# Third and fourth block of a depthwise convolution begun on ScalarE and summed by transfers, and one store on another queue, in a Trainium2 hybrid encoder block

## The chip, the cores and the metric

The kernel runs on one core of one Trainium2 chip, in one launch. The metric is device time in microseconds (us). The engines are named as in the profile: PE is TensorE (its weight loads are PEld), DVE is VectorE, ACT is ScalarE, POOL is GpSimd, SP is SyncE, whose queue starts most loads and stores. Each engine works through its own instructions in the order in which the program lists them, and waits where an operand is not there yet.

## What is computed

One layer of a streaming encoder on 512 tokens of 1,024 channels in fp32: a half-step feed-forward layer, one joint projection whose output feeds a convolution module and a gated linear attention, an output projection, a second half-step feed-forward layer, a gated embedding, and a last norm. The change touches the convolution, in the middle:

```python
def _conv_module(a, b, w_dw, b_dw, ln_g, ln_b):
    glu = a * jax.nn.sigmoid(b)
    y = lax.conv_general_dilated(
        glu, w_dw[:, None, :], window_strides=(1,),
        padding=((CONV_WIDTH - 1, 0),), dimension_numbers=("NWC", "WIO", "NWC"),
        feature_group_count=D_CONV) + b_dw
    return jax.nn.silu(_layernorm(y, ln_g, ln_b))
```

There are 512 channels and a width of 31: each output token is the bias plus 31 products of a channel's own weights with its tokens up to 30 back. The layer norm runs over the 512 channels, so it needs all of them. Beside it the attention works in chunks of 64 tokens with 4 heads; its output is normalised for each head and multiplied by the swish of a gate `r`. Both outputs meet in the output projection `w_out`.

## The kernel before

Channels lie on the 128 partitions, tokens along the row, so the convolution's 512 channels are four blocks of 128 channels by 512 tokens. `glu[c]` is the input of block c and `acc[c]` its accumulator (tiles `cv`). A block is 31 instructions on VectorE (`conv_steps`, lines 1013 to 1020): one `tensor_scalar` that takes the tap without delay and adds the bias, then 30 `scalar_tensor_tensor`, tap w over 512 - (30 - w) columns, which add a product to the accumulator, from 482 columns up to 511. `taps(n)` hands out n such steps at a fixed place in the program, alternating between the two oldest blocks that are not finished. A block that turns out to be finished is dropped, and that call of `taps` counts as one of the n without an instruction. So the taps fill VectorE's time between other work, and the order is written out by hand: PE, DVE and ACT run in the program's order there (`in_order(True)`). GpSimd is not held to that order in this stretch; the scheduler places its instructions.

What stands around the convolution, in order: the projection's blocks for the convolution (`zblock`), whose last gate and value make `glu[3]`; the projections q and k; the tokens' value rows (`tokblock(wv, t)`, tiles `v`); `scores` of the attention, between whose parts `taps((6, 4)[j])` stands and for which GpSimd clears tiles `sc`; then the gate's rows (`tokblock(wr, t)`). After the second of these come 15 taps, the head norm's square sums `so`, and the norm `rso = rsqrt_mean(so, ...)`: a mean `ms` on DVE, its power -1/2 on POOL (`rs<-ms,negh`), five taps, and a Newton step on DVE. ACT multiplies the attention's four token blocks with it (`ytok[i]`, 128 tokens each; the tiles are called `r` or `y` in the profile, after the buffer they share), and DVE multiplies them by the gate's `rt[i]`:

```python
        if t == 3:
            acc012 = bt(s="acc012")
            dve.tensor_tensor(out=acc012, in0=acc[0], in1=acc[1], op=ALU.add)
        if t > 0:
            taps((0, 2, 5, 1)[t])
            for i in {1: (0,), 2: (1, 2), 3: (3,)}[t]:
                dve.tensor_tensor(out=ytok[i], in0=ytok[i], in1=rt[i], op=ALU.mult)
```

TensorE then transposes `ytok[0]` to `ytok[3]` in this order (`ps<-ident,y`), with two products for the later embedding (`sm,px`) ahead of the last. `yg` are the transposed rows scaled, the inputs of `w_out`. All steps of the convolution that are left are run behind `yg`; `acc012`, the sum of the four accumulators (tile `r` in the profile), is multiplied by a constant matrix on TensorE (`ps<-r,mean`), which gives the layer norm's mean.

Products in three parts need each weight split in a rounded part (`wh`, on ACT) and a rest (`wl`). For `added(...)` the rest is made without DVE: ACT writes the negated rounded part and a transfer from POOL's queue adds the weight to it (`accum_op=ALU.add`). Such transfers stand in POOL's queue, and a transfer that waits holds up what is behind it. Weights come through six buffers that SP's loads fill in turn.

At the end each of the four token blocks is stored in two halves of 256 KB (`put`). All go out from SP's queue except `scaled_out(1, 0, ...)`, which is issued on ACT's.

Of the kernel before, what the change touches and what calls it, by code (L numbers as in the profile page):

```python
# [11 lines left out]
AF = mybir.ActivationFunctionType  # L12
ALU = mybir.AluOpType
PSUM = bass.MemoryType.PSUM

P = 128
SEQ = 512
# [4 lines left out]
WIDTH = 31  # L22
PAD = WIDTH - 1
# [39 lines left out]
def block_kernel(ctx: ExitStack, tc: tile.TileContext, a: dict, out: bass.AP):  # L63
    nc = tc.nc
    pe, dve, act, pool = (Ordered(tc, e) for e in (nc.tensor, nc.vector, nc.scalar, nc.gpsimd))
# [15 lines left out]
    def nm(s):  # L81
        uid[0] += 1
        return f"{s}_{uid[0]}"
# [6 lines left out]
    def bt2(dt=F32R, s="a"):  # L90
        t = big.tile([P, 2, SEQ], dt, tag="A", bufs=NA, name=nm(s))
        hi, lo = t[:, 0], t[:, 1]
        whole_of[id(hi)] = hi, t
        return hi, lo

    def bt(dt=F32, s="a"):
        if dt not in other:
            t, other[dt] = bt2(dt, s)
            return t
        return other.pop(dt)  # L100

    def cvt(dt=F32, s="cv"):
        return big.tile([P, SEQ], dt, tag="CV", bufs=NCV, name=nm(s))

    def tmp(s, w=SEQ, dt=F32, bufs=2):
        return tp.tile([P, w], dt, tag=s, bufs=bufs, name=nm(s))
# [20 lines left out]
    def bank():  # L127
        if mode[0] == 0:
            turn_no[0] += 1
            at = turn_no[0] % 7  # L130
            if at in (3, 4):
                return fixed()
            if at in (5, 6):
                return spare()
        return psum(singles(), 3, [P, SEQ])
# [36 lines left out]
    cw = col[:, ncol - DC:]  # L172
# [5 lines left out]
    def vec(name, c, n=1):  # L178
        at = first_of[name] + c
        return col0[:, at:at + n] if at < DC else col[:, at - DC:at - DC + n]  # L180
# [37 lines left out]
    def load(src, k0, nk, c0, ncol):  # L218
        r3 = raw(nk, ncol)
        fetch(r3, src, k0, nk, c0, ncol)  # L220
        return r3

    def high(r3):

        nk, nc_ = r3.shape[1], r3.shape[2]
        hi = wp.tile([P, 1024], F32R, tag="wh", bufs=6, name=nm("wh"))
        lo = wp.tile([P, 1024], F32R, tag="wl", bufs=6, name=nm("wl"))
        h3 = hi[:, :nk * nc_].rearrange("p (k c) -> p k c", k=nk)
        l3 = lo[:, :nk * nc_].rearrange("p (k c) -> p k c", k=nk)
        act.copy(h3, r3)  # L230
        return h3, l3, r3
# [6 lines left out]
    def added(w):  # L238

        h3, l3, r3 = w  # L240
        act.mul(l3, r3, -1.0)
        pool.dma_start(out=l3.bitcast(F32), in_=r3, accum_op=ALU.add)
        return w
# [5 lines left out]
    def mm3(ps, wh, wl, xh, xl, first, last):  # L249
        pe.matmul(ps, wh, xh, start=first, stop=False)  # L250
        pe.matmul(ps, wh, xl, start=False, stop=False)
        pe.matmul(ps, wl, xh, start=False, stop=last)
# [15 lines left out]
    def rows_of(w, k):  # L268

        part, kk = (w[k // 4], k % 4) if isinstance(w, list) else (w, k)  # L270
        return part[0][:, kk, :], part[1][:, kk, :]

    def zblock(w, x, mid={}):

        ps = bank()
        for k in range(DC):
            if k in mid:
                mid[k]()
            wh, wl = rows_of(w, k)
            mm3(ps, wh, wl, *x[k], k == 0, k == DC - 1)  # L280
        return ps
# [728 lines left out]

    glu, acc, conv = [], [cvt() for _ in range(4)], []

    def conv_steps(c):
        y, g, tap = acc[c], glu[c], cw[:, c * WIDTH:(c + 1) * WIDTH]
        dve.tensor_scalar(y, g, tap[:, PAD:WIDTH], vec("conv_b", c), ALU.mult, ALU.add)
        yield
        for w in range(PAD):
            late = PAD - w
            dve.scalar_tensor_tensor(out=y[:, late:], in0=g[:, 0:SEQ - late], scalar=tap[:, w:w + 1],
                                     in1=y[:, late:], op0=ALU.mult, op1=ALU.add)  # L1020
            yield
# [3 lines left out]
    def taps(n):  # L1025

        for _ in range(n):
            if not conv:
                return
            i = turn[0] % min(2, len(conv))  # L1030
            turn[0] += 1
            try:
                next(conv[i])
            except StopIteration:
                conv.pop(i)
# [8 lines left out]
    def glu_value(ps):  # L1044
        a1 = tmp("u1")
        dve.tensor_tensor(out=a1, in0=ps, in1=rsb, op=ALU.mult)
        return a1

    def glu_out(a1, sg):
        g = bt(s="glu")  # L1050
        dve.tensor_tensor(out=g, in0=a1, in1=sg, op=ALU.mult)
        glu.append(g)
        conv.append(conv_steps(len(glu) - 1))
# [77 lines left out]
    cums, epos, eneg, edec, decay, ends = [], [], [], [], [], []  # L1131
    taps(10)
    glu_out(glu_value(pa), sg)
    pb = zblock(w2b[1], hg)
    taps(5)
    for j in range(2):
# [40 lines left out]
    def k_out(j, ps):  # L1177
        for lst, e in ((kdec, edec), (kneg, eneg), (kpos, epos)):
            t = bt(s="k")
            dve.tensor_tensor(out=t, in0=ps, in1=e[j], op=ALU.mult)  # L1180
            lst.append(t)
# [12 lines left out]
    raw_r = [load(a["w_rows"], k, 2, SEQ, SEQ) for k in (0, 2)]  # L1194
# [14 lines left out]
    def tokblock(w, t, mid={}):  # L1209

        ps = bank()
        ts = slice(t * P, (t + 1) * P)
        i = 0
        for k in range(DC):
            wh, wl = w[k // 2][:2]
            xh, xl = hg[k]
            for x, y in ((xh, wh), (xl, wh), (xh, wl)):
                if i in mid:
                    mid[i]()
                pe.matmul(ps, x[:, ts], y[:, k % 2, :], start=(i == 0), stop=(i == 3 * DC - 1))  # L1220
                i += 1
        return ps
# [6 lines left out]
    def scores(j, between):  # L1229
        p4s = [bank().rearrange("p (u c t) -> p u c t", u=2, t=CH) for _ in range(2)]  # L1230
        ss = []
        for i in range(2):
            s = bt(s="sc").rearrange("p (c t) -> p c t", t=P)
            pool.memset(s, 0.0)
            ss.append(s)
        for u, (kk, qq) in enumerate(((kneg[j], qdec[j]), (kpos[j], qneg[j]))):
            for c in range(0, NCH, 2):
                for i in range(2):
                    d = slice(i * HK, (i + 1) * HK)
                    for cc in (c, c + 1):  # L1240
                        s0 = (cc % 2) * CH
                        cs = slice(cc * CH, (cc + 1) * CH)
                        pe.matmul(p4s[i][s0:s0 + CH, u, c // 2, :], kk[d, cs], qq[d, cs], start=True, stop=True)
        hs = [slice(i * CH, (i + 1) * CH) for i in range(2)]
        for s, p4 in zip(ss, p4s):
            for h in hs:
                act.copy(s[h, :, h], p4[h, 0])
        between()
        for s, p4 in zip(ss, p4s):
            for h in hs:  # L1250
                dve.copy_predicated(s[h, :, h], mask[h], p4[h, 1])
        sc.extend(ss)
# [59 lines left out]
    vt, kdt, wr = [], [], []  # L1312
    for t in range(TB):
        ps = tokblock(wv, t, {8: lambda: wr.append(high(raw_r[2])),
                             14: lambda: wr.append(high(raw_r[3]))} if t == 3 else {})
        if t == 0:
            wr += [added(high(raw_r[i])) for i in range(2)]
            k_out(1, k1)
            taps(3)
        elif t == 1:  # L1320
            taps(4)
        elif t == 2:
            taps(3)
        else:
            taps(5)
            low(wr[2])
            taps(2)
            low(wr[3])
        v = bt(s="v")
        act.activation(v, ps, AF.Copy, scale=rs2[:, t:t + 1])  # L1330
        vt.append(v)
        if t == 1:
            for j in range(2):
                scores(j, lambda: taps((6, 4)[j]))
            for j in range(2):
                kp = bank()
                for i in range(TB):
                    pe.transpose(kp[:, i * P:(i + 1) * P], kdec[j][:, i * P:(i + 1) * P], ident)
                kd = bt(s="kdt")
                act.copy(kd, kp)  # L1340
                kdt.append(kd)
# [47 lines left out]
    for t in range(TB):  # L1389
# [21 lines left out]
        if t == 1:  # L1411
# [4 lines left out]
            for i in range(TB):  # L1416
                y = bt(s="y")
# [114 lines left out]
    for k in range(4):  # L1532
        for n in range(3):
            w, ps = half[n]
# [199 lines left out]
    hf, hl = {}, {}  # L1734
# [77 lines left out]
        dve.scalar_tensor_tensor(out=q, in0=r, scalar=nh, in1=r, op0=ALU.mult, op1=ALU.mult)  # L1812
        dve.scalar_tensor_tensor(out=q, in0=q, scalar=1.5, in1=r, op0=ALU.add, op1=ALU.mult)

    def scaled_out(t, e, src, *queue):
        y = bt(s="y")
        act.activation(y, src, AF.Copy, scale=roots[t][2])
        put(t, e, y, *queue)

    def put(t, e, y, queue=nc.sync):  # L1820
        queue.dma_start(out=out[0, t * P:(t + 1) * P, e * SEQ:(e + 1) * SEQ], in_=y)

    def first_half(t, e):
        y = bt(s="y")
# [116 lines left out]
    root(1)  # L1941
    first_half(0, 0)
    scaled_out(0, 1, gained)
    newton(1)
    scaled_out(1, 0, hf[1], act)
    second_half(1, 1)


# [48 lines left out]
```

## Time and profile before

| what | value |
|---|---|
| time, median of 3 runs | 921.92 us (921.84 to 922.2) |
| time of the profiled execution | 921.48 us |
| span of the profiled execution | 919.7 us |
| granted TensorE clock, mean | 0.998 |
| DVE busy, 380 to 480 us | 19.45 to 19.93 of each 20 us |
| ACT busy, 380 to 480 us | 8.19 to 15.82 of each 20 us |

The span runs from the first to the last instruction; the execution's time is 1.8 us longer than it. A line of a timeline gives start, length (us), engine, line, operation, operands, and in brackets the idle time before it and what ended it. All compute instructions pass through one helper, so they have its line, L46, and are told apart by their operands: `cv<-glu,col,cv` is a tap of the second or third block, `cv<-en,col,cv` one of the fourth, whose `glu` shares a buffer named `en`.

### The profile page before, as it was taken

What the parts mean: (1) busy time and instruction counts of PE and PEld (TensorE: products, weight loads), DVE (VectorE), ACT (ScalarE), POOL (GpSimd) and SP (SyncE); (2) the same over time, 40 slices, a digit from 0 to 9 for tenths busy, and PEclk for the clock granted to TensorE, in tenths of its full rate; (3) what the DMA queues carried; (4) which work ended last, traced back from release to release, by engine and by line L of the source; (5) the groups of instructions that cost most, each with busy time, mean ns of one, the idle gap of its engine ahead of it and who ended that gap; (6) DMA issues with size and microseconds to landing.
All of it is one profiled execution on the core that took longest, in us unless ns stands there. A gap on an engine that the chain in (4) does not pass through costs nothing.

```text
span 919.7 us, 12838 instructions
## 1 busy us (share of the span) xinstructions
PE 910.7 (99%) x4948; PEld 779.7 (85%) x4948; DVE 816.7 (89%) x1090; ACT 511.7 (56%) x746; POOL 60.3 (7%) x76
## 2 busy tenths in 40 slices
PE   9999999999999999999999999999999999999996
PEld 8899888888888887788887889888888888888885
DVE  6699989999989766999996779899999999997896
ACT  7755354445454574463665875455445444556884
POOL 0120000000000111001130020000000000000121
PEclk9999999999999999999999999999999999999999
DMA  9534333224334692245572563333223322358454
GB/s 350 186 100 136 117 112 122 91 73 135 115 92 115 158 295 51 69 118 158 139 166 93 137 157 97 115 116 126 87 84 130 122 89 87 118 155 240 92 99 131
DMA packets 37149, 118.89 MB, mean 129 GB/s; under 512 B 4192, under 2 KB 4960, under 8 KB 37088
## 3 DMA queue, kind: packets, MB, share of 16 engines
q1 hardware_dynamic: 30176, 97.22, 31.8%
q0 software_dynamic: 6624, 20.58, 12.5%
q8 instruction: 39, 0.64, 0.3%
q10 hardware_dynamic: 288, 0.27, 0.1%
q14 instruction: 22, 0.18, 0.1%
HBM read 96.43 MB, written 2.10 MB: 107 GB/s over the span
## 4 chain that ended last, share of the span: by engine, by line
PE 96%; DVE 2%; ACT 1%; issue 0%; POOLq 0%
PE ps L46 56%; PE pd L46 40%; DVE cv L46 1%; ACT wa L46 0%; ACT sq L46 0%; DVE yg L46 0%; DVE r L46 0%; DVE y L46 0%; ACT r L46 0%; ACT sm L46 0%; ACT px L46 0%; POOLq L1993 0%; ACT s L46 0%; DVE u L46 0%; DVE g L46 0%
## 5 line engine op out<-in xcount | busy, mean ns | idle before, releaser
L46 DVE TENSOR_TENSOR wl<-wr,wh 128x1024 fp32r<-128x1024 f32 (+2 forms) x159 | 185.9, 1179 | 16.9 <-ACT wh L46 16.4
L46 ACT CAST wh<-wr 128x1024 fp32r<-128x1024 f32 (+2 forms) x177 | 175.4, 1023 | 14.4 <-PE ps L46 7.7
L46 PE MATMUL pd<-hg,wh 128*128 128x512 f32 x576 | 150.0, 391 | 0.0
L46 PE MATMUL ps<-act,wh 128*128 128x512 f32 x448 | 137.9, 389 | 0.0
L46 PEld LDWEIGHTS pd<-hg,wh 128*128 128x128 f32 x576 | 105.9, 188 | 21.1 <-DVE u L46 0.4
L46 PE MATMUL ps<-hg,wh 128*128 128x512 f32 (+1 forms) x448 | 117.0, 345 | 0.0
L46 PEld LDWEIGHTS ps<-act,wh 128*128 128x128 f32 x448 | 84.1, 188 | 17.5
L46 ACT ACTIVATE s<-g 128x512 f32<-128x512 f32 x48 | 30.4, 632 | 117.6 <-DVE g L46 117.6
L46 PE MATMUL pd<-t,wh 128*128 128x512 f32 x392 | 95.3, 391 | 0.0
L46 ACT COPY sq<-pd 128x1024 f32<-128x1024 f32 x45 | 45.8, 1017 | 86.7 <-PE pd L46 52.3
L46 PE MATMUL ps<-act,wl 128*128 128x512 f32 x224 | 87.1, 389 | 0.0
L46 PEld LDWEIGHTS ps<-hg,wh 128*128 128x128 f32 x448 | 78.0, 190 | 10.5 <-issue 0.5
L46 PEld LDWEIGHTS pd<-t,wh 128*128 128x128 f32 x392 | 71.4, 189 | 13.4
L46 PE MATMUL pd<-hg,wl 128*128 128x256 f32 (+1 forms) x544 | 81.5, 289 | 0.0
L46 PEld LDWEIGHTS pd<-hg,wl 128*128 128x128 f32 x544 | 73.9, 191 | 5.1
L46 PE MATMUL ps<-hg,wl 128*128 128x512 f32 (+1 forms) x224 | 77.0, 344 | 0.0
L46 ACT CAST wh<-sm 128x1024 fp32r<-128x1024 f32 x42 | 44.0, 1050 | 55.6 <-DVE sm L46 50.1
L46 DVE TENSOR_TENSOR wl<-sm,wh 128x1024 fp32r<-128x1024 f32 x42 | 51.0, 1219 | 5.1 <-ACT wh L46 5.1
L46 DVE TENSOR_TENSOR sq<-pd,sq 128x1024 f32<-128x1024 f32 x45 | 54.8, 1218 | 0.4 <-PE pd L46 0.4
L46 PE MATMUL ps<-wh,hg 128*128 128x512 f32 x176 | 54.4, 390 | 0.0
L46 PE MATMUL pd<-t,wl 128*128 128x256 f32 x392 | 52.4, 283 | 0.0
L46 PEld LDWEIGHTS pd<-t,wl 128*128 128x128 f32 x392 | 50.6, 191 | 1.5
(300 smaller groups left out, 1625.2 us busy)
## 6 DMA issues: line engine op xcount, KB each, us to landing
wr<-in_ffn_w_in SPq DMA_DIRECT2D x84, 512.0 KB, 3.6
wr<-in_ffn_w_out SPq DMA_DIRECT2D x32, 512.0 KB, 3.6
wl<-wr POOLq DMA_DIRECT2D x20, 512.0 KB, 5.4
wr<-in_ffn_w_out SPq DMA_DIRECT2D x16, 384.0 KB, 3.3
wr<-in_w_blocks SPq DMA_DIRECT2D x12, 512.0 KB, 5.7
wr<-in_w_rows SPq DMA_DIRECT2D x8, 512.0 KB, 3.8
wr<-in_w_out SPq DMA_DIRECT2D x8, 512.0 KB, 5.9
wq<-in_ple_w_gate SPq DMA_DIRECT2D x8, 512.0 KB, 4.3
```

Of the source, the lines that this page charges most:

```text
L46: inst = call(*args, **kwargs)
```

## The change

`taps_begin` lets ACT write the biased tap into `acc[2]` and `acc[3]`. `taps_apart` lets ACT write the product of one tap into a tile of its own, and `taps_add` adds such a tile to another or to the accumulator by a transfer from POOL's queue. `APART` says how many taps of each block are done so: two for the third, five for the fourth. `conv_steps` leaves these out. Separately, `scaled_out(1, 0, ...)` is now issued on SP's queue like the others.

```diff
+    def taps_apart(c, w, y):
+        late = PAD - w
+        act.activation(y[:, late:], glu[c][:, 0:SEQ - late], AF.Copy, scale=cw[:, c * WIDTH + w:c * WIDTH + w + 1])
+        return y
+    def taps_begin(c):
+        act.activation(acc[c], glu[c], AF.Identity, bias=vec("conv_b", c), scale=cw[:, c * WIDTH + PAD:(c + 1) * WIDTH])
+    def taps_add(y, x, w):
+        pool.dma_start(out=y[:, PAD - w:], in_=x[:, PAD - w:], accum_op=ALU.add)
+    APART = (0, 0, 2, 5)
     def conv_steps(c):
         y, g, tap = acc[c], glu[c], cw[:, c * WIDTH:(c + 1) * WIDTH]
-        dve.tensor_scalar(y, g, tap[:, PAD:WIDTH], vec("conv_b", c), ALU.mult, ALU.add)
-        yield
-        for w in range(PAD):
+        if not APART[c]:
+            dve.tensor_scalar(y, g, tap[:, PAD:WIDTH], vec("conv_b", c), ALU.mult, ALU.add)
+            yield
+        for w in range(APART[c], PAD):
...
     glu_out(glu_value(pa), sg)
+    taps_begin(2)
+    ta = [taps_apart(2, w, bt(s="ta")) for w in range(2)]
+    taps_add(ta[1], ta[0], 0)
+    taps_add(acc[2], ta[1], 1)
     pb = zblock(w2b[1], hg)
...
         if t == 0:
-            wr += [added(high(raw_r[i])) for i in range(2)]
+            wr.append(added(high(raw_r[0])))
+            taps_begin(3)
+            ta = [taps_apart(3, w, tmp(("g1", "u1", "s")[w])) for w in range(3)]
+            taps_add(acc[3], ta[0], 0)
+            taps_add(ta[2], ta[1], 1)
+            wr.append(added(high(raw_r[1])))
+            ta += [taps_apart(3, w, tmp(("g1", "u1")[w - 3])) for w in (3, 4)]
+            taps_add(acc[3], ta[3], 3)
+            taps_add(ta[4], ta[2], 2)
             k_out(1, k1)
             taps(3)
...
                 scores(j, lambda: taps((6, 4)[j]))
+                if j == 0:
+                    taps_add(acc[3], ta[4], 4)
...
-    scaled_out(1, 0, hf[1], act)
+    scaled_out(1, 0, hf[1])
```

The numbers of taps that each `taps(n)` hands out are as they were, and so is the order of TensorE's instructions. On VectorE every tap of the third block moves up by three and of the fourth by six. The first place shown is VectorE between the head norm's last step and the multiplication of `ytok[3]`. There `cv_3195` is the third block's accumulator, `cv_3196` the fourth's, the last column the columns of the tap; `r<-r,st` multiplies `ytok[0]`, the three `y` rows multiply `ytok[1]`, `ytok[2]` and `ytok[3]`, and `r<-cv_3193,cv_3194` adds the first two accumulators. Before:

```order
L46 SCALAR_TENSOR_TENSOR cv_3196<-en_3562,col,cv_3196 128x498
L46 SCALAR_TENSOR_TENSOR cv_3195<-glu_3512,col,cv_3195 128x509
L46 TENSOR_TENSOR r_4271<-r_4271,st_4123 128x512
L46 SCALAR_TENSOR_TENSOR cv_3196<-en_3562,col,cv_3196 128x499
L46 SCALAR_TENSOR_TENSOR cv_3195<-glu_3512,col,cv_3195 128x510
L46 SCALAR_TENSOR_TENSOR cv_3196<-en_3562,col,cv_3196 128x500
L46 SCALAR_TENSOR_TENSOR cv_3195<-glu_3512,col,cv_3195 128x511
L46 SCALAR_TENSOR_TENSOR cv_3196<-en_3562,col,cv_3196 128x501
L46 TENSOR_TENSOR y_4297<-y_4297,r_4271 128x512
L46 TENSOR_TENSOR y_4297<-y_4297,y_4306 128x512
L46 TENSOR_TENSOR r_4372<-cv_3193,cv_3194 128x512
L46 TENSOR_TENSOR y_4306<-y_4306,r_4372 128x512
```

At the same place on VectorE, in the changed kernel:

```order
L46 SCALAR_TENSOR_TENSOR cv_3196<-en_3568,col,cv_3196 128x504
L46 TENSOR_TENSOR r_4293<-r_4293,st_4145 128x512
L46 SCALAR_TENSOR_TENSOR cv_3196<-en_3568,col,cv_3196 128x505
L46 SCALAR_TENSOR_TENSOR cv_3196<-en_3568,col,cv_3196 128x506
L46 SCALAR_TENSOR_TENSOR cv_3196<-en_3568,col,cv_3196 128x507
L46 SCALAR_TENSOR_TENSOR cv_3196<-en_3568,col,cv_3196 128x508
L46 SCALAR_TENSOR_TENSOR cv_3196<-en_3568,col,cv_3196 128x509
L46 TENSOR_TENSOR y_4319<-y_4319,r_4293 128x512
L46 TENSOR_TENSOR y_4319<-y_4319,y_4328 128x512
L46 TENSOR_TENSOR r_4393<-cv_3193,cv_3194 128x512
L46 SCALAR_TENSOR_TENSOR cv_3196<-en_3568,col,cv_3196 128x510
L46 TENSOR_TENSOR y_4328<-y_4328,r_4393 128x512
```

One tap fewer stands ahead of `ytok[0]`, the five behind it are all of the fourth block, and one tap stands ahead of `ytok[3]` that was not there. The second place is GpSimd from the attention's value rows on. Before (`wl` are rests of weights, `sc` the cleared tiles):

```order
L46 DMA wl_3591<-wr_3346 128x1024
L46 DMA wl_3805<-wr_3688 128x1024
L46 DMA wl_3810<-wr_3690 128x1024
L46 MEMSET sc_3855 128x512 x2
L46 MEMSET sc_3906 128x512 x2
```

At the same place on GpSimd, in the changed kernel (`g`, `u` and `s` are the partial products of the fourth block):

```order
L46 DMA wl_3811<-wr_3694 128x1024
L46 DMA cv_3196<-g_659_3816 128x482
L46 DMA s_3820<-u_660_3818 128x483
L46 DMA wl_3825<-wr_3696 128x1024
L46 DMA cv_3196<-g_664_3829 128x485
L46 DMA u_665_3831<-s_3820 128x484
L46 MEMSET sc_3876 128x512 x2
L46 MEMSET sc_3928 128x512 x2
L46 DMA cv_3196<-u_665_3831 128x486
```

Four adding transfers now stand ahead of the memsets, and a fifth behind them. The third place is GpSimd around the head norm's power. Before (`px` and `sm` belong to the later embedding, `wa` to `w_out`):

```order
L46 DMA wl_4047<-wr_4042 128x1024
L46 DMA wl_4052<-wr_4044 128x1024
L46 DMA px_4041<-u_680_4038 128x256
L46 TENSOR_TENSOR rs_710_4256<-ms_4254,negh 128x16
L46 DMA sm_4234<-wr_4036 128x1024
```

At the same place on GpSimd, in the changed kernel:

```order
L46 DMA wl_4069<-wr_4064 128x1024
L46 DMA wl_4074<-wr_4066 128x1024
L46 DMA px_4063<-u_686_4060 128x256
L46 DMA sm_4256<-wr_4058 128x1024
L46 TENSOR_TENSOR rs_716_4278<-ms_4276,negh 128x16
```

The power and the transfer of `sm` have changed places.

More of the change, by code (lines that the diff above doesn't have):

```diff
@@ L1813, in newton, with scaled_out, put @@
         dve.scalar_tensor_tensor(out=q, in0=q, scalar=1.5, in1=r, op0=ALU.add, op1=ALU.mult)
-    def scaled_out(t, e, src, *queue):
+    def scaled_out(t, e, src):
         y = bt(s="y")
         act.activation(y, src, AF.Copy, scale=roots[t][2])
-        put(t, e, y, *queue)
-    def put(t, e, y, queue=nc.sync):
-        queue.dma_start(out=out[0, t * P:(t + 1) * P, e * SEQ:(e + 1) * SEQ], in_=y)
+        put(t, e, y)
+    def put(t, e, y):
+        nc.sync.dma_start(out=out[0, t * P:(t + 1) * P, e * SEQ:(e + 1) * SEQ], in_=y)
     def first_half(t, e):
```

## The prediction

> **What bounds the kernel now.** I read the page first (its span and the busy row), then TensorE's table of waits, then the timelines of TensorE, VectorE, ScalarE and GpSimd around the third and fourth block of the convolution.
>
> ```profile
> span 919.7 us, 12838 instructions
> PE 910.7 (99%) x4948; PEld 779.7 (85%) x4948; DVE 816.7 (89%) x1090; ACT 511.7 (56%) x746; POOL 60.3 (7%) x76
> PE ps L46 <- PEq L1987: 0.8, 1, 0.8
> PE ps L46 <- DVE r L46: 0.3, 1, 0.3
> ```
>
> TensorE is busy for 910.7 of 919.7 us, and its table of waits has two rows: 0.8 us at the start of the program and 0.3 us for a VectorE tile `r`. So nothing taken from VectorE can be worth much by itself: only the places count where TensorE stands, and places where it newly would stand. There are two such places beside the convolution, and both lie in one stretch of TensorE's timeline (start, us, operation, operands):
>
> ```profile
> 470.45 1.19 PE L46 MATMUL ps<-ident,y 128*128 128x128 f32 x8
> 471.39 0.71 PE L46 MATMUL ps<-sm,px 128*128 128x512 f32 x2
> 472.19 0.66 PE L46 MATMUL ps<-ident,y 128*128 128x128 f32 x4
> 479.18 4.24 PE L46 MATMUL ps<-yg,wa 128*128 128x512 f32 x18
> 483.72 1.12 PE L46 MATMUL ps<-r,mean 128*128 128x512 f32 x2 [0.30 <-DVE r L46]
> 482.97 0.70 DVE r L46
> ```
>
> The first place is the turning of the attention's output. `ps<-ident,y` transposes the tokens' rows `ytok[1]` and `ytok[2]` (x8) and `ytok[3]` (x4), which VectorE has just multiplied. The second is the mean of the convolution, `ps<-r,mean`: `r` is the sum of the four accumulators, and the last row, from the chain of waits, shows VectorE's last addition to it starting at 482.97. The 18 products ahead of the mean start every (4.24 - 0.39) / 17 = 0.227 us, where 0.39 us is the length of a single one in that timeline; the mean's slot is then 479.18 + 18 x 0.227 = 483.27, and it starts at 483.72. **That stall, 0.45 us, is all that the convolution's length costs**; up to 0.1 more is lost between the mean's two passes, so 0.5.
>
> **The change, part by part.** *Nine instructions leave VectorE:* two biased taps (TENSOR_SCALAR) and seven ordinary ones. Here are the rows that price them.
>
> ```profile
> 412.18 0.54 DVE L46 TENSOR_SCALAR cv<-glu,col 128x512 f32<-128x512 f32 x1
> 412.63 2.02 DVE L46 SCALAR_TENSOR_TENSOR cv<-glu,col,cv 128x502 f32<-128x502 f32 x3
> 433.30 0.54 DVE L46 TENSOR_SCALAR cv<-en,col 128x512 f32<-128x512 f32 x1
> 433.87 1.84 DVE L46 COPY_PREDICATED sc<-mask,ps 64x256 f32<-64x256 int32 x4
> 463.93 0.38 DVE L46 SCALAR_TENSOR_TENSOR rs<-rs,rs 128x16 f32<-128x16 f32 x2
> 465.75 0.69 DVE L46 TENSOR_TENSOR r<-r,st 128x512 f32<-128x512 f32 x1
> 468.33 0.74 DVE L46 SCALAR_TENSOR_TENSOR cv<-glu,col,cv 128x511 f32<-128x511 f32 x1
> 468.99 0.73 DVE L46 SCALAR_TENSOR_TENSOR cv<-en,col,cv 128x501 f32<-128x501 f32 x1
> 469.64 0.68 DVE L46 TENSOR_TENSOR y<-y,r 128x512 f32<-128x512 f32 x1
> 471.45 0.68 DVE L46 TENSOR_TENSOR y<-y,r 128x512 f32<-128x512 f32 x1
> 475.94 4.64 DVE L46 SCALAR_TENSOR_TENSOR cv<-en,col,cv 128x503 f32<-128x503 f32 x6
> ```
>
> Taps on two accumulators in turn start about 0.65 us apart (468.33 to 468.99), although each lasts 0.74. Taps that follow each other on one accumulator start (4.64 - 0.75) / 5 = 0.78 us apart: the next waits until the last has ended. The code hands out a fixed number of taps at each place, so the nine that go are missing at the end: those from 475.94 to 482.97, which is 7.0 us. The sum `r` would be ready near 478 instead of 483.7. The stall at the mean goes: **-0.5 us**. Nothing is late behind it, since the mean's inputs then lead by 5 us.
>
> The Trainium skill ("VectorE: DVE Perf Modes", Terms) says that every VectorE instruction ends in a flush and that the next cannot issue before the pipe is empty. Alternating taps here overlap by 0.08 us, so by these rows that holds only for the tap that depends on the one before; by the rule the grouping of taps would cost nothing, step (2) below would be zero, and the sum would give 922.4.
>
> *What is late instead.* The rows of the order show that the places between the taps are unchanged but the taps in them are not, and `ytok[3]` is paid for that in three steps.
>
> (1) Ahead of the attention's norm, VectorE is later by: 0.18 (the biased tap's slot, 412.18 to 412.63 = 0.45, now holds a tap of 0.63 to 0.65), 0.07 (the slot at 433.30, 0.57 long, likewise), and about 0.15 for taps that are longer by three and by six columns (some 40 of them; an estimate from 0.54 us for 512 columns: 0.001 us a column, 159 columns). That is 0.4. Then the norm's power on GpSimd:
>
> ```profile
> 458.79 1.18 ACT L46 ACTIVATE sm<-wr 128x1024 fp32r<-128x1024 f32 x1
> 464.48 1.24 ACT L46 ACTIVATE r<-ps,rs 128x128 f32<-128x128 f32 x4
> 417.86 0.86 POOL L46 DMA_DIRECT2D wl<-wr  x1 [4.20 <-ACT wl L46]
> 418.40 1.33 POOL L46 MEMSET sc<- 128x512 f32 x2
> 460.12 3.35 POOL L46 TENSOR_TENSOR rs<-ms,negh 128x16 f32<-128x16 f32 x1 [0.90 <-DVE ms L46]
> 463.44 0.91 POOL L46 DMA_DIRECT2D sm<-wr  x1
> ```
>
> The order puts the power behind the transfer of `sm`, which needs ScalarE's `sm` (done 458.79 + 1.18 = 459.97) and holds GpSimd for 0.54 (417.86 to 418.40) to 0.9. The power so starts at 460.5 to 460.9, not 460.12, and with its 3.35 us the last root is done 0.4 to 0.75 late, at 464.7 to 465.1 (463.93 + 0.38 = 464.31 now). ScalarE scales `ytok[0]` from 464.48, with 0.17 to spare; VectorE multiplies it at 465.75, having waited. So `ytok[0]` moves by 0.25 to 0.6: **+0.45**. The tap less that now stands ahead of it doesn't help, since VectorE waits there anyway.
>
> (2) Between `ytok[0]` and `ytok[1]` stand five taps. Now they alternate; then the third block is finished and all five are on the fourth, four of them right behind one another: 4 x (0.78 - 0.65) = **+0.5**.
>
> (3) Between `ytok[2]` and `ytok[3]` a tap now comes that wasn't there (in its place the code met a finished block): 469.64 - 468.99 = **+0.65**.
>
> `ytok[3]`, at 471.45 now, then comes 1.6 late, and its transposes, which already start right behind it (471.45 + 0.68 = 472.13, 472.19), move from 472.19 to about 473.8. TensorE has nothing to put there: its queue is in order, the two `sm,px` products ahead are done. **+1.6 us**. Bounds: 0 if all three are covered by something I don't see, 1.8 with the upper end of (1). Behind them the scaling and the products of `yg` follow as before.
>
> *Nine activations go to ScalarE*, two of them biased.
>
> ```profile
> 396.94 0.63 ACT L46 ACTIVATE s<-g 128x512 f32<-128x512 f32 x1 [6.01 <-DVE g L46]
> 411.44 1.06 ACT L46 ACTIVATE wl<-wr 128x1024 fp32r<-128x1024 f32 x1
> 415.56 1.05 ACT L46 CAST wh<-wr 128x1024 fp32r<-128x1024 f32 x1 [3.05 <-PE ps L46]
> 421.18 0.69 ACT L46 ACTIVATE v<-ps,rs 128x512 f32<-128x512 f32 x1 [3.61 <-PE ps L46]
> 427.78 3.05 ACT L46 COPY sc<-ps 64x256 f32<-64x256 f32 x8 [0.48 <-PE ps L46]
> ```
>
> At 0.69 us at most each, three fit (2.1) in the 6.01 us that ScalarE idles ahead of 396.94, four (2.8) in the 3.05 ahead of 415.56, two (1.4) in the 3.61 ahead of 421.18: **0 us**. Without that cover the `v` copies, and TensorE's banks, would be late by the difference.
>
> *Seven adding transfers go to GpSimd's queue*, two chained for block three, five for block four (accumulator, one partial sum, accumulator, partial sum, accumulator), each waiting for the landing of an earlier one. No row has such a transfer of 240 KB; the nearest are those of 256 KB:
>
> ```profile
> wa<-wr POOLq DMA_DIRECT2D x12, 256.0 KB, 5.5
> DMA to landing us min/median/max: 3.9/5.5/10.4
> ```
>
> Block three's start near 391.5 and are needed at 412.18: 20 us for two. Block four's first can start near 413.9 (ScalarE's row at 411.44 ends 412.50, then two activations); the last of three in a row lands, by the median, at 413.9 + 16.5 = 430.4 and is needed by the first tap at 433.5. By three minima it is 425.6, by three maxima 445. I take the median: **0 us**, 3 us to spare. Behind the waiting transfers on GpSimd stand the `sc` memsets: they would move from 418.40 to about 422 to 425, and are needed at 427.78; the second pair already waits for VectorE.
>
> The Trainium skill ("DMA: Bandwidth & Descriptors", Anatomy of one DMA) gives 2.0 us plus bytes over 436 GB/s: an estimate of 2.6 us here, so the last would land at 421.7. The rows are twice that; by the page alone the rival on late transfers would have no chance.
>
> *The last store but one moves from ScalarE's queue to SP's.*
>
> ```profile
> 915.98 0.38 ACTq L46 DMA_DIRECT2D out<-y  x1
> out<-y ACTq DMA_DIRECT2D x1, 256.0 KB, 2.8
> out<-y SPq DMA_DIRECT2D x1, 256.0 KB, 2.6
> L1821 SPq DMA_DIRECT2D out<-y x6: 332/332/399, 908.1 to 916.0; - x6
> DMA to landing us min/median/max: 2.1/2.3/2.8
> ```
>
> Both last stores are issued at 916.0 and land 2.6 and 2.8 later, at 918.8. From one queue the second is issued 0.35 later and lands after 2.1 to 2.8: 918.45 to 919.15, with the median 918.65. **-0.1**, between -0.3 and +0.4.
>
> **Sum:** +1.6 - 0.5 - 0.1 = +1.0 us. The profiled execution took 921.48 (1.8 beside its span), which gives 922.5; the median of the runs, 921.92, is 0.44 above that execution, so **922.9 us**. A measurement of this kernel can tell some 0.2% (1.84 us) from no change: the forecast is "within 0.2%".
>
> **Rivals.** *The lateness doesn't arrive.* If the three steps are hidden, or the tap counts shift otherwise than I read, only the gains are left: 0.5 and 0.1, and at most the 0.4 us that TensorE now loses at 470.98 and 472.19; 920.9 to 921.4. For it: VectorE has 5.9 us less to do. Against: all of them lie behind the places that wait. Chance 0.21.
>
> *The adding transfers are late.* From 433.5 on VectorE stands for the landing of block four's last one, and nothing later gives the time back before `ytok[3]`, because VectorE is busy throughout; each us of that wait beyond the first 0.3 (which GpSimd's power already costs) is a us for TensorE. It decides when three landings take more than 433.5 - 413.9 = 19.6 us in all, and passes 0.2% when they take over 20.7, 6.9 each. For it: in the row above one landing took 10.4, and the first two share the queue with 512 KB transfers issued at 412.80 and 417.86. One at 10.4 and two at 5.5 make 21.4: 1.8 us of wait, +2.5 in sum: 924.4. Chance 0.19.
>
> *The change gains over 0.2%*: that needs 1.9 us of TensorE's stalls, more than the rows have. 0.03.
>
> **How the numbers follow.** Forecast 0.57 (922.0 to 923.7), rivals 0.21, 0.19 and 0.03. Within 0.2%: 0.57 + 0.21 = 0.78; slower 0.19; faster 0.03. The range takes in most of both rivals: 921.0 to 924.4.
>
> **What would show it.** In the new profile the mean's product has no wait; `ytok[3]`'s transposes wait for VectorE over 1 us; `rs<-ms,negh` starts behind the transfer of `sm`; the five taps ahead of `ytok[1]` stand 0.78 apart; the first tap of block four starts near 433.5 with no wait for a transfer. I am wrong if that tap waits, if ScalarE's `v` or `sc` copies start later, or if the transposes don't move.

## The result, and the profile after

| | before | after |
|---|---|---|
| time, median of 7 runs each | 921.92 us (921.63 to 922.83) | 924.72 us (924.44 to 927.68) |
| ratio, 95% interval | | 1.0038 [1.0027, 1.0048] |
| time of the profiled execution | 921.48 us | 924.44 us |
| span of the profiled execution | 919.7 us | 922.7 us |

By the medians the changed kernel is slower by 2.8 us, 0.3%, and 0.3 us above the forecast's range. The profiled execution is the fastest of its seven, so the stalls read from it may be smaller than those of the median. The page of the changed kernel (span and busy times), and below it TensorE's and VectorE's tables of waits (total us, times, longest):

```profile
span 922.7 us, 12853 instructions
PE 911.4 (99%) x4948; PEld 780.1 (85%) x4948; DVE 811.1 (88%) x1081; ACT 517.4 (56%) x755; POOL 66.2 (7%) x83
PE ps L46 <- DVE y L46: 2.1, 2, 1.3
PE ps L46 <- PEq L2016: 0.8, 1, 0.8
PE ps L46 <- DVE st L46: 0.8, 1, 0.8
DVE cv L46 <- DMA cv<-u: 1.1, 1, 1.1
```

VectorE is indeed 5.6 us less busy (816.7 to 811.1), and TensorE's wait for `r` is gone. In its place TensorE has three new waits: two for the attention's rows `y`, forecast, and one for the state `st`, which the forecast did not name. The last line points to the source of that one: VectorE stood 1.1 us for block four's last adding transfer.

Where the 3.0 us of span come from is read by comparing the starts of the same products in TensorE's two timelines, a few rows of each, before first:

```profile
448.44 3.73 PE L46 MATMUL ps<-v,sc 128*128 128x128 f32 x32
470.01 0.60 PE L46 MATMUL ps<-ident,r 128*128 128x128 f32 x4
484.28 1.95 PE L46 MATMUL ps<-yg,wa 128*128 128x512 f32 x6
911.68 0.28 PE L46 MATMUL ps<-wl,s 128*128 128x256 f32 x1
```

And TensorE's timeline after:

```profile
448.91 0.38 PE L46 MATMUL ps<-v,sc 128*128 128x128 f32 x2
450.08 3.14 PE L46 MATMUL ps<-v,sc 128*128 128x128 f32 x26 [0.79 <-DVE st L46]
471.51 0.60 PE L46 MATMUL ps<-ident,r 128*128 128x128 f32 x4
473.46 1.26 PE L46 MATMUL ps<-ident,y 128*128 128x128 f32 x8 [1.35 <-DVE y L46]
475.93 0.66 PE L46 MATMUL ps<-ident,y 128*128 128x128 f32 x4 [0.74 <-DVE y L46]
482.92 4.25 PE L46 MATMUL ps<-yg,wa 128*128 128x512 f32 x18
487.01 1.02 PE L46 MATMUL ps<-r,mean 128*128 128x512 f32 x2
487.47 1.94 PE L46 MATMUL ps<-yg,wa 128*128 128x512 f32 x6
914.85 0.28 PE L46 MATMUL ps<-wl,s 128*128 128x256 f32 x1
```

Each difference is a lag so far: 0.47 at the first `v,sc` (this arises in the first 20 us, ahead of any change, and differs between the profiles), 1.50 at `ident,r`, 3.74 at the 18 products of `yg,wa` (479.18 before), 3.19 behind the mean, 3.17 at the last product, 3.0 at the end. The steps between are the stalls: **state +1.03, rows +2.24, mean -0.55, last store -0.17.**

Rows of VectorE's timeline of the changed kernel show where the first two come from:

```profile
435.15 0.72 DVE L46 SCALAR_TENSOR_TENSOR cv<-en,col,cv 128x487 f32<-128x487 f32 x1 [1.11 <-DMA cv<-u]
448.82 1.38 DVE L46 SCALAR_TENSOR_TENSOR st<-st,decay,ps 128x128 f32<-128x128 f32 x5
...
468.94 3.87 DVE L46 SCALAR_TENSOR_TENSOR cv<-en,col,cv 128x505 f32<-128x505 f32 x5
...
474.53 0.74 DVE L46 SCALAR_TENSOR_TENSOR cv<-en,col,cv 128x510 f32<-128x510 f32 x1
475.19 0.68 DVE L46 TENSOR_TENSOR y<-y,r 128x512 f32<-128x512 f32 x1
```

The first tap of block four waits for its transfer. VectorE is in order, so all that follows is late, first of all the state's steps, five of which stood at this place before:

```profile
446.74 1.37 DVE L46 SCALAR_TENSOR_TENSOR st<-st,decay,ps 128x128 f32<-128x128 f32 x5
```

They start 2.08 later, 1.61 beyond the 0.47 (0.39 in the version without this transfer, below), and TensorE's `v,sc` products stand for the state. Then come the five taps in a row on one accumulator (468.94) and the tap between the last rows (474.53), both as forecast.

GpSimd's timeline shows the chain of transfers. The names are those of the buffers: `g`, `u` and `s` hold the products, `cv` is the accumulator. A row gives the issue alone, and the bracket what it waited for:

```profile
414.54 0.86 POOL L46 DMA_DIRECT2D cv<-g  x1 [0.43 <-ACT g L46]
415.72 0.86 POOL L46 DMA_DIRECT2D s<-u  x1 [0.32 <-ACT s L46]
421.08 0.86 POOL L46 DMA_DIRECT2D cv<-g  x1 [1.89 <-DMA cv<-g]
423.46 0.86 POOL L46 DMA_DIRECT2D u<-s  x1 [1.51 <-DVE cv L46]
431.83 0.86 POOL L46 DMA_DIRECT2D cv<-u  x1 [5.57 <-DMA u<-s]
462.06 0.86 POOL L46 DMA_DIRECT2D sm<-wr  x1 [1.33 <-ACT sm L46]
462.64 3.64 POOL L46 TENSOR_TENSOR rs<-ms,negh 128x16 f32<-128x16 f32 x1
```

And the profile's view of the transfers, in two stretches. The first is 413 to 436 us: the bandwidth in 40 equal slices, the rows of GpSimd's queue and of SP's (q0 and q1: packets, MB, share of the 16 DMA engines' time), and each issue's size and time to landing. Then come block three's two, from 391 to 402 us:

```profile
GB/s 271 178 349 378 285 249 207 184 187 183 169 188 190 228 269 322 303 289 242 292 271 256 299 342 345 259 238 243 241 307 328 256 157 14 14 149 183 102 0 0
q0 software_dynamic: 1008, 2.29, 56.9%
q1 hardware_dynamic: 918, 2.84, 33.1%
wr<-in_w_out SPq DMA_DIRECT2D x3, 512.0 KB, 8.3
cv<-u POOLq DMA_DIRECT2D x1, 243.0 KB, 3.3
cv<-g POOLq DMA_DIRECT2D x1, 242.5 KB, 9.0
u<-s POOLq DMA_DIRECT2D x1, 242.0 KB, 7.8
s<-u POOLq DMA_DIRECT2D x1, 241.5 KB, 7.0
cv<-g POOLq DMA_DIRECT2D x1, 241.0 KB, 6.0
...
cv<-ta POOLq DMA_DIRECT2D x1, 241.5 KB, 3.3
ta<-glu POOLq DMA_DIRECT2D x1, 241.0 KB, 4.1
```

Read them as a sum. The second transfer, issued at 415.72, lands after 7.0, at 422.7; the fourth adds to its result, is issued at 423.46 and lands after 7.8, at 431.3; the fifth is issued at 431.83 and lands at 435.1, where VectorE's tap starts. The first and third, 6.0 and 9.0, end earlier, at 430.1. (The bracket of the fourth names a tap of VectorE; but in every profile that has this transfer its issue follows the landing of the second by 0.5 to 0.8 us.) The same transfer that takes 6.0 to 9.0 us here takes 3.3 where little else moves: the last one has the queues nearly to itself (the slices around 433 us hold 14 GB/s, then its own 149 and 183). Block three's two landed after 4.1 and 3.3 us, each with about one transfer of 512 KB beside it.

What moves beside block four's is not weights' loads alone. GpSimd's own queue takes more of the engines' time than SP's, 56.9% to 33.1%, and from 416 to 419 us it moves 0.56 MB where SP's moves 0.02: there the first two transfers share the engines with a weight's rest of 512 KB on their own queue, issued at 413.25. The loads come in behind.

### The profile page after: what moved, and what is told of

Its sections match the earlier page's. It is cut to its first block, busy times and chain, and to the rows that moved or that the text cites. A ratio compares the mean times of both kernels' runs of the same rounds, so it can differ in the third digit from the quotient of the medians.

```text
span 922.7 us, 12853 instructions
## 1 busy us (share of the span) xinstructions
PE 911.4 (99%) x4948; PEld 780.1 (85%) x4948; DVE 811.1 (88%) x1081; ACT 517.4 (56%) x755; POOL 66.2 (7%) x83
## 4 chain that ended last, share of the span: by engine, by line
PE 96%; DVE 2%; ACT 1%; POOL 0%; issue 0%; POOLq 0%
PE ps L46 56%; PE pd L46 40%; DVE cv L46 1%; ACT sq L46 0%; DVE y L46 0%; POOL rs L46 0%; DVE st L46 0%; ACT r L46 0%; ACT wa L46 0%; DVE r L46 0%; ACT sm L46 0%; DVE rs L46 0%; DVE wl L46 0%; DVE pq L46 0%; ACT px L46 0%
```

## The experiments

The kernel before stood beside each group of runs: 921.98 us for the first four, 921.87 for the next four, 922.11 for the last two. In the first four, theory A is that the time comes from VectorE's wait for the last transfer and from the places of the taps and of the power among the attention's rows; from the fifth on, each expectation says what its A and B are.

**Without the last adding transfer.**

```diff
-                if j == 0:
-                    taps_add(acc[3], ta[4], 4)
```

> The last adding transfer of block four is left out, so the products of its taps 1, 2 and 4 are missing from the sum; all other instructions stay. Theory A (the transfers' queue): VectorE's wait of 1.11 us at the first tap of block four is the cause of TensorE's stall at the attention's value products (0.95 us) and of part of the one at ytok; without it the first stall is zero, ytok[3] comes about 1.6 us later than before the change, and the time is about 922.9. Theory B (load: seven more transfers and nine more activations slow their neighbours wherever they run): the wait is a symptom, six of seven transfers are still there, and the time stays near 924.4.

Measured 923.04 us (922.73 to 923.78), ratio 1.0012 [1.0003, 1.0022]. Block four's first tap starts at 433.63 without a wait, TensorE's wait for `st` is gone, those for the rows stay, 1.16 and 0.74. So one transfer of 243 KB is worth 924.72 - 923.04 = 1.7 us by the medians, through the wait for it, and what is left is the forecast's sum.

**Block three alone.** `taps_begin(3)` and all of block four's products and transfers go.

```diff
-    APART = (0, 0, 2, 5)
+    APART = (0, 0, 2, 0)
```

> Only block three is begun on ScalarE (APART = 0, 0, 2, 0). Theory A: no wait for a transfer and no stall at the value products; the five taps ahead of ytok[1] are all on block four and stand 0.78 apart, and a tap stands ahead of ytok[3], so its transposes come 1.2 to 1.3 later than before; the stall at the mean (0.56) and 0.17 at the end are gained: 922.5. Theory B (cost in proportion to the transfers, two of seven): 922.7. This run separates them only by the place of the stall.

Measured 922.45 us (921.89 to 922.74), 1.0005 [0.9996, 1.0015]. This run separates the three steps at the rows, since here GpSimd's power stands ahead of the transfer of `sm`. VectorE's timeline of it:

```profile
466.63 0.69 DVE L46 TENSOR_TENSOR r<-r,st 128x512 f32<-128x512 f32 x1 [0.57 <-ACT r L46]
...
471.00 0.69 DVE L46 TENSOR_TENSOR y<-y,r 128x512 f32<-128x512 f32 x1
473.46 0.69 DVE L46 TENSOR_TENSOR y<-y,r 128x512 f32<-128x512 f32 x1
```

And of the version without the last transfer, where the power stands behind it:

```profile
466.80 0.69 DVE L46 TENSOR_TENSOR r<-r,st 128x512 f32<-128x512 f32 x1 [0.55 <-ACT r L46]
...
471.19 0.69 DVE L46 TENSOR_TENSOR y<-y,r 128x512 f32<-128x512 f32 x1
473.66 0.69 DVE L46 TENSOR_TENSOR y<-y,r 128x512 f32<-128x512 f32 x1
```

Subtract from each the time of before (465.75, 469.64, 471.45 for `ytok[0]`, `ytok[1]`, `ytok[3]`) and the lag that TensorE already had at `v,sc` (449.32 - 448.44 = 0.88 in block three alone, 448.60 - 448.44 = 0.16 without the last transfer):

| late by, us | `ytok[0]` | `ytok[1]` | `ytok[3]` | TensorE's loss, `ident,r` to `yg,wa` |
|---|---|---|---|---|
| block three alone | 0.00 | 0.48 | 1.13 | 1.11 |
| without the last transfer | 0.89 | 1.39 | 2.05 | 2.05 |

Step (2) is the column's step from 0.00 to 0.48 (and 0.89 to 1.39), step (3) the next, 0.65 and 0.66, and both arrive at TensorE whole. Step (1) is 0 with the power ahead and 0.89 with it behind, but the order is not all of it. Less the lag, VectorE's `ms` is late by 0.21 in the first version and by 0.48 in the second, since only the second begins block four on ScalarE: 0.27 of the 0.89. The power then starts 0.22 later behind `ms` (0.48 in place of 0.26) and takes 3.77 us in place of 3.36.

**Block four alone.** `taps_begin(2)` and block three's two products and transfers go.

```diff
-    APART = (0, 0, 2, 5)
+    APART = (0, 0, 0, 5)
```

> Only block four is begun on ScalarE (APART = 0, 0, 0, 5). Block three's taps are where they were, so the five taps ahead of ytok[1] alternate again and no tap stands ahead of ytok[3]. Theory A: VectorE still waits about 1 us for the last transfer, TensorE stalls about 0.9 at the value products, but ytok[1] follows ytok[0] by 3.9 us as before and ytok[3] by 5.7; 923.2 in all. Theory B (five of seven transfers): 923.9, with the stall at ytok as in the changed kernel.

Measured 923.27 us (922.5 to 926.05), 1.0019 [1.001, 1.0028]. The profiled execution was the longest of them, 926.05. VectorE's table of waits there:

```profile
DVE cv L46 <- DMA cv<-u: 4.4, 1, 4.4
```

Four times the wait of the changed kernel's profile, with the same five transfers: its fourth landed after 10.1 us and the fifth was issued at 435.18. TensorE stood 1.6 us for `st` and 1.7 for the low parts of weights (`wl`) that VectorE makes. The price of this wait is no constant. The rows behave as A has them: `ytok[1]` follows `ytok[0]` by 3.90 us and `ytok[3]` by 5.70 as before, TensorE waits there only 0.2 us, and between `ident,r` and `yg,wa` it loses 0.46 in place of 2.24.

**The taps handed out later**, so that none stands ahead of the last row and fewer ahead of the second.

```diff
-            taps((0, 2, 5, 1)[t])
+            taps((0, 2, 1, 0)[t])
```

> The changed kernel with five of the taps between ytok[0] and ytok[3] moved behind them (2, 1 and 0 taps instead of 2, 5 and 1), where VectorE has 6 us to spare ahead of the mean. Theory A: the stall at the value products stays (0.95), the ones at ytok[1] and ytok[3] (1.5 and 0.9) go but for some 0.3, and the mean doesn't wait: 922.3. Theory B: unchanged, 924.7.

Measured 922.96 us (922.53 to 924.68), 1.0015 [1.0006, 1.0025]. The rows' stalls are gone but for 0.25 us (from `ident,r` to `yg,wa` the lag grows from 2.83 to 3.08), and the mean has no wait. But the wait for the last transfer is 2.9 us in this profile, and TensorE stands 1.56 us for `st` and 0.7 for the low parts of weights. Expected were 922.3 by A and 924.7 by B; the time lies between, nearer to A, and the taps' places are worth the 924.72 - 922.96 = 1.8 us that the two versions are apart. The range of 2.2 us within one kernel fits a wait that varies, but only one of its executions has a profile.

**The store alone**, in the kernel before.

```diff
-    scaled_out(1, 0, hf[1], act)
+    scaled_out(1, 0, hf[1])
```

> The kernel before, with the one store moved to SP's queue and nothing else. Theory A (what the changed kernel's tail shows, 7.88 us from TensorE's last product to the end of the span where it was 8.05, is the store): the tail is 7.9 us and the time 921.8 us, 0.15 under the kernel before. Rival B (the shorter tail is the scatter between two executions): the tail stays at 8.0 to 8.1 us and the time at 922.0.

Measured 921.73 us (921.23 to 922.21), 0.9998 [0.9989, 1.0007]. In the trace the last product starts at 911.63 and the span ends at 919.5: 7.9 us, as A has it. The times agree with -0.15 (921.87 to 921.73), but the interval alone would not tell it from nothing.

**Block three alone, with one tap fewer ahead of each of the last two groups of rows.**

```diff
-    APART = (0, 0, 2, 5)
+    APART = (0, 0, 2, 0)
...
-            taps((0, 2, 5, 1)[t])
+            taps((0, 2, 4, 0)[t])
```

> Block three alone begun by ScalarE, and the taps between the attention's rows handed out as 2, 4, 0 in place of 2, 5, 1, so that no tap stands ahead of the last row that stood behind it before. Theory A (block three's transfers cost nothing, and the taps' places cost all of the 1.0 us that the block three version lost against what it freed): TensorE has no wait for the rows' turning beyond 0.3 us and none at the mean, and the time is 921.98 - 0.55 - 0.15 = 921.3 us. Rival B (the activations and transfers of block three take something of their own): 921.9 us or more, with a wait of TensorE elsewhere.

Measured 920.98 us (920.52 to 921.25), 0.9989 [0.9981, 0.9998]: below A's 921.3, and the lowest median of all. TensorE waits for neither the rows nor the mean, and its lag is 0.10 at `ident,r`, -0.18 at `yg,wa`, -0.73 behind the mean, -0.75 at the last product. No cost of block three's transfers is seen; 1.5 us of the time of its sister version (922.45) were the places of two taps.

**A chain of two transfers in block four.** Three taps apart, the second link issued ahead of all but the first of the four cleared score tiles.

```diff
-    APART = (0, 0, 2, 5)
+    APART = (0, 0, 2, 3)
...
             taps_add(acc[3], ta[0], 0)
             taps_add(ta[2], ta[1], 1)
             wr.append(added(high(raw_r[1])))
-            ta += [taps_apart(3, w, tmp(("g1", "u1")[w - 3])) for w in (3, 4)]
-            taps_add(acc[3], ta[3], 3)
-            taps_add(ta[4], ta[2], 2)
+            taps_add(acc[3], ta[2], 2)
...
-                if j == 0:
-                    taps_add(acc[3], ta[4], 4)
...
-            taps((0, 2, 5, 1)[t])
+            taps((0, 2, 1, 0)[t])
```

> Both blocks, but three taps of block four apart instead of five, so that two transfers follow each other there instead of three, the second issued ahead of the cleared score tiles; the taps between the rows are 2, 1, 0. Theory A (what costs is the length of the chain of landings, some 8 us each from about 414): the last landing is near 430 to 432, VectorE's first tap of block four near 433.6 waits for no transfer, the state chain ends as it did before, TensorE has no wait for it, and what is left is the power behind the transfer of sm, +0.5 at the rows' turning: 921.98 - 0.55 - 0.15 + 0.5 = 921.8 us, with a spread of about 1 us. Rival B (any adding transfers in this stretch are late, however few, since the queue is full of weights there): VectorE waits over 1 us for the last, and the time is 922.9 us with a spread of 2 us or more.

Measured 921.34 us (920.77 to 921.98), 0.9992 [0.9983, 1.0001], 1.2 us between the ends. The second link is issued at 423.46 and lands after 7.5, at 431.0. VectorE's timeline:

```profile
433.55 0.72 DVE L46 SCALAR_TENSOR_TENSOR cv<-en,col,cv 128x485 f32<-128x485 f32 x1
466.69 0.69 DVE L46 TENSOR_TENSOR r<-r,st 128x512 f32<-128x512 f32 x1 [0.56 <-ACT r L46]
470.36 0.69 DVE L46 TENSOR_TENSOR y<-y,y 128x512 f32<-128x512 f32 x1 [1.73 <-ACT y L46]
```

The tap waits for nothing, B falls. The three landings (6.2, 7.6 and 7.5) are no shorter than in the changed kernel: two transfers fewer did not speed up the others, the chain only has a link less. There is a second reading: `ytok[0]` is late by 466.69 - 465.75 - 0.06 = 0.88 here too, for the power again stands behind `sm`, and TensorE loses nothing between `ident,r` and `yg,wa` (0.06 to 0.10). With one tap behind `ytok[0]` in place of five, VectorE has 1.73 us to wait for ScalarE there anyway. So in these runs step (1) costs only where taps fill the room behind it, and my +0.5 for it in this version was wrong.

**The power ahead of the transfer of `sm`**, tried by writing the copies for `sm` behind the norm, on the chain of two and on the version without the last transfer.

```diff
             ps = tokblock(wr, t, {2: outputs})
-            early_parts()
             taps(15)
...
+            early_parts()
         else:
```

> The version with a chain of two transfers, and in addition the copies that feed the transfer of sm are written behind the norm of the attention, so that GpSimd's power stands ahead of that transfer as it did before. Theory A (the power behind the transfer costs the first row 0.4 us, and the rows' turning waits for it): the power starts right behind VectorE's ms, TensorE's wait at the rows goes, and the time is 0.4 us under the version without this edit: 921.4 us. Rival B (the first row has that much to spare, and what is left of the wait comes from the taps ahead of it): the same time as that version.

> The version without the last adding transfer (it leaves out three taps of block four), and in addition the copies that feed the transfer of sm are written behind the attention's norm, so that GpSimd's power stands ahead of that transfer, as it did in the kernel before. Step (1) of the prediction (the power behind the transfer makes the first row late, and the rows' turning with it): the power starts right behind VectorE's ms, the first row is 0.4 to 0.75 us earlier, TensorE's waits for the rows go from 1.3 and 0.9 to 1.7 in all, and the time is 922.5 us, 0.5 under the version without this edit. Rival (the first row has that to spare, as it had in the version with a chain of two, and only the taps ahead of the second and the last row count): the waits stay, and the time is 923.0.

Measured 921.17 us (920.65 to 921.71) and 923.03 us (922.86 to 923.77), ratios 0.9992 [0.9983, 1.0001] and 1.0012 [1.0004, 1.0021]. Neither says anything on step (1): the edit moved no instruction. In both traces the transfer of `sm` is still issued ahead of the power (460.64 and 460.65, the power at 461.20 and 461.22). They serve as repeats: 921.34 and 921.17 of the one version, 923.04 and 923.03 of the other.

**The transfers as plain copies.**

```diff
-        pool.dma_start(out=y[:, PAD - w:], in_=x[:, PAD - w:], accum_op=ALU.add)
+        pool.dma_start(out=y[:, PAD - w:], in_=x[:, PAD - w:])
```

> The changed kernel with the seven transfers of blocks three and four as plain copies of the same bytes in the same places, so the partial sums are not added up. Theory A (they land late because the stretch is full of weights, whatever they do): landings of block four stay near 6, 7, 9, 8 and 3 us, VectorE waits for the last one, and the time is 924.7 us. Rival B (it is the adding that is slow, since the destination is read as well): landings near 5 us, no wait of VectorE at block four's first tap, TensorE waits for no state, and the time is 923.0 us.

Measured 923.10 us (922.85 to 923.58), 1.0013 [1.0004, 1.0022]: B's time. All seven transfers are there, and the time is that of the version without the last one (923.04). In the view of the transfers from 405 to 440 us, first the row of GpSimd's queue (packets, MB, share of the 16 engines), then the landings:

```profile
q0 software_dynamic: 742, 2.77, 32.9%
cv<-u POOLq DMA_DIRECT2D x1, 243.0 KB, 2.9
cv<-g POOLq DMA_DIRECT2D x1, 242.5 KB, 6.1
u<-s POOLq DMA_DIRECT2D x1, 242.0 KB, 6.2
s<-u POOLq DMA_DIRECT2D x1, 241.5 KB, 7.1
cv<-g POOLq DMA_DIRECT2D x1, 241.0 KB, 7.3
```

The same row of the changed kernel, in the same stretch:

```profile
q0 software_dynamic: 1152, 2.81, 45.4%
```

Half of each theory holds. Plain copies take 6 to 7 us in this stretch and 2.9 alone, so the other traffic doubles them, adding or not. The first two are no faster as plain copies (7.3 and 7.1 against 6.0 and 7.0), and of block three's two one is faster and one slower (3.3 and 3.6 against 4.1 and 3.3). But the third takes 9.0 us adding against 6.1, the fourth 7.8 against 6.2, the fifth 3.3 against 2.9, and in the profiles of the other kernels that have them, the adding third and fourth take 8.7 to 9.5 and 7.7 to 10.1. Adding occupies the engines for 45.4% of the stretch in place of 32.9%, with nearly the same bytes. The last link is issued at 429.85 in place of 431.83 and lands at 432.8, 0.9 us ahead of the tap (433.67). Without the adding the chain is in time; with it, it is not. How the share of the traffic divides between the loads of weights, the weights' rests on GpSimd's queue and the chain's own transfers was not tried.

## Why the prediction was wrong, step by step

**The step that failed is the term of the adding transfers: "I take the median: 0 us, 3 us to spare".** I took three landings of 5.5 us, the median of twelve transfers of 256 KB elsewhere in the program, back to back from the first at 413.9. The critical chain began with the second, at 415.72, and its landings were 7.0, 7.8 and 3.3 us, with 0.5 to 0.8 us from a landing to the next issue; it ended at 435.1, not 430.4. Of these 4.7 us the later start is 1.8 (0.45 of it the lag that this execution had already), the landings are 1.6, and the two gaps, which I had put at nothing, are 1.3. The landings alone, put right, would have ended at 432.0 and met the tap.

What I had set down as the rival was right, in place and in kind: VectorE stands at 434.0 for block four's last transfer, beyond the 19.6 us from 413.9 (21.2 were taken), and that is the first of the signs of being wrong that I had named. That its price came out nearly right, 924.4 against 924.72, is in part luck. It had one landing of 10.4 and two of 5.5 without gaps, a wait of 1.8 us worth 1.5 to TensorE; the profile has a wait of 1.1, worth 1.2, beside a step (1) that is 0.4 larger than forecast. I had put the rival at one value and ended the range there, though its own bounds of three maxima ran to 445; the waits measured were 1.1, 2.9 and 4.4 us in the profiles of three kernels.

By the formula of the Trainium skill ("DMA: Bandwidth & Descriptors", Anatomy of one DMA) I had estimated 2.6 us for such a transfer. Alone, the plain copy took 2.9 and the adding one 3.3; in this stretch the estimate is short by a factor of 2.3 to 3.5, and it spoke for the wrong case.

The way of the wait to TensorE was incomplete. I named the rows; the trace shows the state first, and TensorE pays 1.03 us there of VectorE's 1.61, since the state had 0.6 to spare. At the rows only 0.19 more is lost than without the wait (2.24 to 2.05).

**The rest of the sum held, with one part mis-sized.** Without the wait the kernel takes 923.04, forecast 922.9. The two are this close because a step (1) that was too small and gains that were slightly too small offset each other in part.

- Step (1), the power behind `sm`: +0.45 forecast, 0.89 measured. This is the mis-sized part. GpSimd's power starts 0.7 later (forecast 0.4 to 0.8), and takes 3.49 to 3.79 us there in place of 3.35, which I had kept.
- Step (2), the five dependent taps: +0.5 forecast, 0.48 and 0.50 measured. This bears on the rule of the Trainium skill ("VectorE: DVE Perf Modes", Terms) that each instruction's flush ends before the next issues: by it step (2) would be zero. For alternating taps, 0.65 apart and 0.74 long, the rule does not hold here.
- Step (3), the tap ahead of `ytok[3]`: +0.65 forecast, 0.65 and 0.66 measured.
- The mean: -0.5 forecast, -0.55 measured. The last store: -0.1 forecast, -0.17 in the changed kernel, and about -0.15 by itself.
- Nine activations: 0 forecast. The two biased ones took 0.80 us each, not 0.69 at most, and still no wait of TensorE for ScalarE appears in any table of waits.
- Block three's transfers: 0 forecast, none seen; they landed by 400.2 and were needed at 412.6.

In the traces the sum without the wait is 2.05 - 0.55 - 0.17 = +1.3 us, by the medians 923.04 - 921.98 = +1.1; the forecast was +1.0.

## What to carry to other kernels

A chain of dependent transfers is priced link by link: when its own first link can start, how long each landing takes among all that moves in that stretch, on its own queue too, and the gap from a landing to the next issue. A median over the program had none of the three; here 3.3 us alone became 6 to 9, and a deadline that a chain of two met was missed by a chain of three, by a different amount in each of three profiles. When work leaves an in-order engine whose instructions are handed out by count, the instructions behind it move up into other gaps: here the counts (5, 1) changed to (4, 0) turned block three's version from 922.45 to 920.98 us, the lowest median of the study. A rival with bounds of its own belongs into the range with those bounds.

## What the runs showed of the hardware

- Adding transfers of 242 KB on GpSimd's queue landed after 3.3 us with little else under way, after 3.3 to 4.2 with about one transfer of 512 KB beside them, after 5.9 to 10.1 in the busy stretch from 414 us on. Plain copies of the same bytes took 2.9, 3.3 to 3.6, and 6.1 to 7.3.
- Issuing an adding transfer holds GpSimd for 0.86 us, a plain one between the same buffers for 0.54 to 0.57.
- Three kernels with the same five transfers in block four waited 1.1, 2.9 and 4.4 us for the last of them, in one profile each. These kernels spread over 2.2 to 3.6 us in time, the versions without the wait over 0.7 to 1.2 (the kernel before over up to 1.8, in its largest group of runs).
- GpSimd's power on 16 columns took 3.35 to 3.36 us ahead of the issue of a transfer, and 3.49 to 3.79 right behind one.
